# Down projection of a transformer block in seven products over halves, its summed activations made while gate and up are computed

## The chip, the cores and the metric

One core of one Trainium2 chip runs the whole block. The metric is the device time of one execution in microseconds (us), the median of several runs. The engines are TensorE (PE, with its weight loads as PEld), VectorE (DVE), ScalarE (ACT), GpSimd (POOL) and SyncE (SP), whose queue issues the DMAs of this kernel.

## The reference, cut to what matters

The block has a Hyena branch, a differential attention branch, an output projection and, last, a SwiGLU feed-forward. The change lies in the feed-forward alone:

```
hf = modulate(rmsnorm(x, g_ffn_pre), sh2, sc2)                      # 1024 positions x 1024
f  = (silu(hf @ w_gate) * (hf @ w_up)) @ w_down                     # 1024 x 2816, then 2816 x 1024
x  = x + g2 * rmsnorm(f, g_ffn_post)
```

All of it is in float32. Each product of two float32 matrices is computed as three matmuls on rounded halves: with a = a_hi + a_lo (a_hi rounded to TensorE's fp32r form, a_lo the rest), the kernel takes hi x hi, lo x hi and hi x lo. Making a hi takes one ScalarE copy, making a lo one VectorE subtraction.

## The kernel before

The kernel is written in a tile framework: code states tiles, rings of buffers (a tag with `bufs` slots) and operations. When the kernel is built, a list scheduler gives each engine its order by a model of the times, with the program's order as priority; on the chip each engine and the SP queue then run in that fixed order, each instruction waiting for what it needs. Loads are often issued far ahead of the place where the code states them, as far as a free slot of their ring allows.

The feed-forward has three stages around the change.

**Gate and up** (lines 1271 to 1370). The hidden size 2816 is NF = 22 tiles of 128. The result is computed transposed, hidden units on partitions, positions along the free axis in halves of 512. Tiles i and i + 11 (NH2 = 11) of gate (even j) and up (odd j) are taken together, and the 2 x 2 block product over halves of hidden units and of positions is made in seven products instead of eight, with sums of the weights made on VectorE (`prep`) and sums of the activations made once (`combos`). `product` runs 12 matmuls for each: 4 contraction tiles x 3 terms. `order` is (1, 5, 6, 3, 7, 2, 4); for the first NHS = 12 j's products 1 and 2 were made in an earlier head part that runs while the second half of the positions is still being prepared, so `order1` is (5, 6, 3, 7, 4). Several products accumulate on the same PSUM bank after its earlier content was copied out (b1, b5). `out_block(j, q, ...)` ends a block q (0, 1: first hidden half, 2, 3: second; even and odd: first and second half of positions): for gate it applies Silu, for up it calls `hidden`, which multiplies the two (VectorE), rounds the product to hi (ScalarE, line 1208), subtracts (VectorE) and stores both halves to DRAM (`ad[0]`, `ad[1]`). The weights come in as `wraw` tiles from a ring of 2 and are split into `whi` and `wlo` one product ahead (LA = 1).

**Down** (lines 1425 to 1459). For each half n of the positions and each half z of the outputs, 11 pieces q of two hidden tiles each are multiplied into four PSUM banks, one for each block b of 128 positions. A piece is `rows`: 4 blocks x 2 tiles x 3 terms = 24 matmuls with 512 output columns; a position block of the activations is the stationary operand, the weights move. `Pieces` loads w_down (512-byte runs, line 1032), splits 1024 columns at a time (line 126, line 127) and runs one piece ahead. The activations come back from DRAM already split (`down_load`), once for each n, into free slots of the rings xc, hfb, hfa and hfc. In all that is 2 x 2 x 11 x 24 = 1056 matmuls.

**End** (lines 1384 to 1467). `end_block` takes a finished bank: ScalarE sums the squares, VectorE multiplies by the gain (`om`). With both z done, `rows_rstd` makes the reciprocal root (12 small VectorE operations) and `turn` transposes back into feature-major form by small matmuls, adds x and stores. For n = 0 this (`final0`) runs between the pieces of n = 1. For n = 1 the last NLAST = 5 pieces of z = 1 are run block by block, so that the end of one block stands beside the matmuls of the next.

Of the kernel before, what the change touches and what calls it, by code (L numbers as in the profile page):

```python
# [17 lines left out]
P = 128  # L18
# [45 lines left out]
def block_kernel(tc, xT, ctxT, cvec, cT, wada1, wada, vecs, lamv, dbias, zT, fw1, fw2, fv, fw3, decay, mfs, mis, rope,  # L64
# [953 lines left out]
    ad = [[dp.tile([P, L], F32R, name=f"ad{j}{m}") for m in range(NF)] for j in range(2)]  # L1018
# [167 lines left out]


    KS2 = []
    for i in range(0, NH2 - 1, 2):
        KS2 += [(i, i + 1), (i + NH2, i + NH2 + 1)]  # L1190
    KS2.append((NH2 - 1, NF - 1))
    A_of = [{}, {}]

    def down_load(n, i):

        if n == 0:
            ring = (rt, "xc", 16) if i < 8 else (gp, "hfb", 16) if i < 16 else (rt, "hfa", 16)
        else:
            ring = (rt, "hfa", 16) if i < 2 else (fc, "hfc", 24) if i < 14 else (rt, "xc", 16)
        A_of[n][i] = split_tile(*ring)  # L1200
        for j in range(2):
            rawdma(A_of[n][i][j], ad[j][KS2[i // 2][i % 2]][:, n * 512:(n + 1) * 512])
# [22 lines left out]
    def out_block(j, q, t, hi=None):  # L1225


        i, mat = j // 2, j % 2
        if mat == 0:
            blk[i, q] = t if hi is None else hi  # L1230
            act(blk[i, q], t, AF.Silu)
        else:
            hidden(blk.pop((i, q)), t, t if hi is None else hi, i + NH2 * (q // 2), slice(q % 2 * 512, q % 2 * 512 + 512))
# [66 lines left out]
    pieces = [(n, z, q) for n in range(2) for z in range(2) for q in range(NH2)]  # L1300
    wd = Pieces(wdown, [(z, KS2[q]) for n, z, q in pieces])

# [5 lines left out]
    for g, (j, p) in enumerate(flat):  # L1308
# [21 lines left out]
        if j == NF - 1 and p in (7, 2):  # L1330
            wd.load()
            if p == 2:
                wd.split()
        product(b, wset.pop(g), XT[p], p in (1, 5) or (p == 2 and not head) or (p == 6 and j < NHS))
        ring = (lambda: xc("kp")) if j < NHS else p1_tile
# [3 lines left out]
        elif p == 2 and head:  # L1339
            out_block(j, 0, b, c11_tile())  # L1340
# [10 lines left out]
        elif p == 6:  # L1351
            keep[6] = evict(ring, b, "e")
        elif p == 3:
            tt(keep[6], keep[6], b, ALU.add)
            out_block(j, 1, keep[6])
        elif p == 7:
            if j < NHS:
                f7 = ring()
                tt(f7, p1[j], b, ALU.add)
            else:  # L1360
                f7 = evict(ring, b, "f")
            tt(keep[5], keep[5], f7, ALU.add)
            out_block(j, 3, keep[5])
        elif j < NHS:
            tt(p1[j], p1[j], b, ALU.add)
            out_block(j, 2, p1.pop(j))
        else:
            out_block(j, 2, b, ring())
        if 14 <= j < 18 and p in (5, 2):
            down_load(0, 2 * (j - 14) + (p == 2))  # L1370
# [32 lines left out]
    def final0():  # L1403
        scale_rows(0, rows_rstd(ssq[:, 2], D))
        yield
        for b in range(4):
            turn(0, b, bank2)
# [11 lines left out]
    def end_block(n, b, z, src):  # L1419
        sq = gp.tile([P, 512], F32, tag="c11", bufs=NC11, name="sq")  # L1420
        act(sq, src, AF.Square, accum_out=ssq[:, 2 + n, b, z:z + 1])
        om[n, b, z] = gp.tile([P, 512], F32, tag="p1", bufs=NHS, name="om")
        tt(om[n, b, z], src, gbc[z], ALU.mult)

    NLAST = 5
    kept = []
    for n, z, q in pieces:
        if (n, z) == (1, 1) and q >= NH2 - NLAST:
            kept.append(wd.next(len(kept) < 1) if len(kept) < 2 else
                        wd.keep(lambda: rt.tile([P, 512], F32R, tag="hfa", bufs=16, name="wkeep")))  # L1430
            continue
        if q == 0:
            acc = [bank() for b in range(4)]
        rows(acc, wd.next(), [A_of[n][2 * q + kk] for kk in range(2)], q == 0, q == NH2 - 1)
        if n == 0 and z == 0:
            if q < 4:
                for i in range(8 + 4 * q, min(12 + 4 * q, NF)):
                    down_load(0, i)
            else:
                for i in range(2):  # L1440
                    down_load(1, 2 * (q - 4) + i)
            if q == 3:
                down_gain()
        if n == 0 and z == 1 and 5 <= q < 9:
            for i in range(2):
                down_load(1, 14 + 2 * (q - 5) + i)
        if n == 1 and z == 0:
            if q == 0:
                load_x2(0)
                next(done)  # L1450
            elif q in (3, 4, 5, 6):
                next(done)
            elif q == 8:
                load_x2(1)
        if q == NH2 - 1:
            for b in range(4):
                end_block(n, b, z, acc[b])
            if z == 1:
                done = final0()

    for b in range(4):
        for i, w in enumerate(kept):
            q = NH2 - NLAST + i
            rows(acc, w, [A_of[1][2 * q + kk] for kk in range(2)], False, i == NLAST - 1, (b,))
        end_block(1, b, 1, acc[b])
        r = rows_rstd(ssq[:, 3, b:b + 1], D)
        turn(1, b, bank2, r)
# [103 lines left out]
```

## Time and profile before

| | |
|---|---|
| median of 3 runs | 1845.4 us (1843.83 to 1846.57) |
| profiled execution, its own time | 1844.04 us |
| its span from first to last instruction | 1842.3 us (1.7 us lie around it) |
| mean granted TensorE clock | 0.981 |
| TensorE busy, matmuls | 1750.0 us (95%), 8122 matmuls |
| VectorE busy | 1242.9 us (67%) |
| ScalarE busy | 752.6 us (41%) |

A matmul's busy time is longer than the distance to the next one, since matmuls overlap; how many end in a stretch says how fast TensorE runs. An idle time of an engine is put down to whatever released it last. The clock column tells which share of full speed TensorE was granted; 1.00 is 2.4 GHz, and the lower of its two levels is 1.2 GHz.

### The profile page before, as it was taken

How to read it: one execution, taken by the hardware profiler on the slowest of the kernel's cores; microseconds unless marked ns; L12 is line 12 of the kernel's file. 1: busy time of each engine (PE TensorE's matmuls, PEld its weight loads, DVE VectorE, ACT ScalarE, POOL GpSimd, SP SyncE). 2: the span in 40 equal slices, each digit the busy share in tenths (PEclk: the TensorE clock that was granted, in tenths of full speed). 3: DMA queues.
4: the chain of work that ended last, by engine and by line, in shares of the span. 5: the costliest groups of instructions: out<-in, count | busy, mean ns of one | idle time of the engine just before them, and what ended most of it. 6: DMA issues, size and time to landing. Idle time of an engine off the chain costs nothing.

```text
span 1842.3 us, 22476 instructions
## 1 busy us (share of the span) xinstructions
PE 1750.0 (95%) x8122; PEld 1404.0 (76%) x8122; DVE 1242.9 (67%) x2213; ACT 752.6 (41%) x1177; POOL 58.2 (3%) x63
## 2 busy tenths in 40 slices
PE   7899999999996999999998899989999999999997
PEld 3488777787875888887876687767778888788886
DVE  4887786777768589898858647876776565323334
ACT  3512323222232376667756357633334444222221
POOL 0000000000000211120100000000000000000000
PEclk9999999999997999999999899999999999999999
DMA  9244533324267733436438753433435324987432
GB/s 330 95 168 168 194 120 124 111 98 154 81 218 235 235 114 124 132 109 216 135 133 298 233 166 116 137 119 120 138 122 199 113 92 149 322 255 210 138 91 69
DMA packets 190111, 293.92 MB, mean 160 GB/s; under 512 B 15235, under 2 KB 110223, under 8 KB 188720
## 3 DMA queue, kind: packets, MB, share of 16 engines
q1 hardware_dynamic: 183776, 284.82, 47.0%
q10 hardware_dynamic: 6224, 7.66, 1.4%
q8 instruction: 64, 1.05, 0.3%
q14 instruction: 47, 0.39, 0.1%
HBM read 213.78 MB, written 78.64 MB: 159 GB/s over the span
## 4 chain that ended last, share of the span: by engine, by line
PE 70%; DVE 17%; DMA 7%; ACT 3%; issue 2%; SPq 0%; ACTq 0%; DVEq 0%
PE pj L1181 19%; PE ps L134 16%; PE ps L1043 15%; DVE pair L77 4%; PE S L804 4%; DVE quad L77 3%; PE pt L826 2%; PE psf L392 2%; PE psf L393 2%; DVE wlo L77 1%; PE psf L537 1%; PE pv L835 1%; PE psf L576 1%; PE psf L378 1%; DMA wraw<-wupf 1%
## 5 line engine op out<-in xcount | busy, mean ns | idle before, releaser
L77 DVE TENSOR_TENSOR wlo<-wraw,whi 128x1024 fp32r<-128x1024 f32 (+1 forms) x192 | 180.7, 949 | 286.8 <-ACT whi L126 130.9
L126 ACT CAST whi<-wraw 128x1024 fp32r<-128x1024 f32 (+1 forms) x119 | 118.1, 993 | 200.4 <-PE ps L1043 164.0
L134 PE MATMUL ps<-h_hi,wlo 128*128 128x512 f32 x640 | 173.6, 401 | 0.7 <-DVE wlo L77 0.7
L134 PE MATMUL ps<-h_hi,whi 128*128 128x512 f32 x640 | 173.9, 402 | 0.4 <-ACT h_hi L438 0.2
L134 PE MATMUL ps<-h_lo,whi 128*128 128x512 f32 x640 | 166.9, 393 | 0.0
L134 PEld LDWEIGHTS ps<-h_hi,wlo 128*128 128x128 f32 x640 | 119.4, 190 | 24.9 <-DVE wlo L77 1.1
L134 PEld LDWEIGHTS ps<-h_hi,whi 128*128 128x128 f32 x640 | 119.4, 191 | 24.1 <-ACT h_hi L438 1.2
L134 PEld LDWEIGHTS ps<-h_lo,whi 128*128 128x128 f32 x640 | 119.0, 188 | 24.1
L1181 PE MATMUL pj<-hfc,whi 128*128 128x512 f32 x528 | 131.7, 391 | 0.2 <-ACT p L1216 0.2
L1181 PEld LDWEIGHTS pj<-hfc,whi 128*128 128x128 f32 x528 | 98.9, 188 | 22.8 <-ACT p L1216 0.7
L804 PE MATMUL S<-KS,Q 128*128 128x512 f32 (+1 forms) x384 | 108.1, 377 | 2.9 <-DVE pr L808 2.7
L486 ACT COPY gt<-ps 128x512 f32<-128x512 f32 x56 | 32.9, 588 | 186.5 <-PE ps L134 149.2
L1181 PE MATMUL pj<-hfb,whi 128*128 128x512 f32 x352 | 93.4, 403 | 9.2 <-ACT whi L1173 9.2
L1181 PE MATMUL pj<-hfa,whi 128*128 128x512 f32 x352 | 90.1, 395 | 0.2 <-ACT whi L1173 0.2
L1181 PEld LDWEIGHTS pj<-hfb,whi 128*128 128x128 f32 x352 | 66.6, 191 | 27.5 <-ACT whi L1173 12.3
L804 PEld LDWEIGHTS S<-KS,Q 128*128 128x128 f32 x384 | 65.4, 191 | 16.8 <-DVE pr L808 9.0
L1181 PEld LDWEIGHTS pj<-hfa,whi 128*128 128x128 f32 x352 | 65.5, 188 | 15.5 <-ACT whi L1173 1.2
L1173 ACT CAST whi<-s 128x512 fp32r<-128x512 f32 x66 | 40.5, 621 | 77.0 <-DVE s L77 56.9
L1173 ACT CAST whi<-wraw 128x512 fp32r<-128x512 f32 x88 | 52.8, 618 | 44.7 <-PE pj L1181 34.0
L1181 PE MATMUL pj<-hfc,wlo 128*128 128x512 f32 x264 | 70.6, 389 | 0.0
L77 DVE TENSOR_TENSOR quad<-psf,xb 128x512 f32<-128x512 f32 x64 | 41.0, 682 | 35.9 <-ACT xb L250 35.9
L77 DVE TENSOR_TENSOR al<-pt,ah 128x512 fp32r<-128x512 f32 x80 | 52.2, 684 | 11.0 <-ACT ah L830 10.2
(492 smaller groups left out, 3566.4 us busy)
## 6 DMA issues: line engine op xcount, KB each, us to landing
wraw<-win SPq DMA_DIRECT2D x46, 512.0 KB, 4.1
wraw<-wdown SPq DMA_DIRECT2D x88, 256.0 KB, 3.4
wada_t<-wada SPq DMA_DIRECT2D x32, 512.0 KB, 8.0
wraw<-wgate SPq DMA_DIRECT2D x28, 512.0 KB, 3.3
wraw<-wupf SPq DMA_DIRECT2D x28, 512.0 KB, 3.9
ad<-p SPq DMA_DIRECT2D x52, 256.0 KB, 2.3
w_ada<-wada SPq DMA_DIRECT2D x16, 512.0 KB, 7.2
kspec<-quad SPq DMA_DIRECT2D x8, 1024.0 KB, 3.9
```

Of the source, the lines that this page charges most:

```text
L77: (eng or V).tensor_tensor(out=out, in0=a, in1=b, op=op)
L126: A.copy(out=hi, in_=raw)
L134: T.matmul(out=ps, lhsT=w[:, k * P:(k + 1) * P], rhs=xs[k][j], start=start and i == 0, stop=stop and i == len(seq) - 1)
L378: T.matmul(out=ps, lhsT=a[:, cs], rhs=b, start=i == 0, stop=i == 2)
L392: T.matmul(out=out, lhsT=mfm(part, r), rhs=gen[r][:, 0:256], start=True, stop=False)
L393: T.matmul(out=out, lhsT=mfm(pb, rb), rhs=gen[rb][:, 256:512], start=False, stop=True)
L486: A.copy(out=gt, in_=ps)
L804: T.matmul(out=S[:, :cn], lhsT=Q[j][:, i, qt * P:(qt + 1) * P], rhs=KS[i][:, c0:c0 + cn], start=j == 0, stop=j == 1)
L826: T.transpose(out=pt[:, b * 256 + qt * P:b * 256 + (qt + 1) * P], in_=av[qt][:, kt * P:(kt + 1) * P], identity=ident)
L1043: T.matmul(out=acc[b].rearrange("p (m c) -> p m c", m=4), lhsT=xs[kk][i == 1][:, b * P:(b + 1) * P], rhs=w[i == 2][kk], start=first and (k ...
L1173: A.copy(out=hi, in_=src)
L1181: T.matmul(out=ps, lhsT=w[a][:, k * P:(k + 1) * P], rhs=xs[k][b], start=start and i == 0, stop=stop and i == 11, skip_group_check=True)
```

## The change

The down product is treated as the gate and up products are: positions (n), hidden units (h: tiles i and i + 11) and outputs (z) are each cut into halves, and the 2 x 2 block product is made in seven products of 11 tiles each, in the order PR = (5, 1, 6, 7, 4, 3, 2). Each is 11 tiles x 4 blocks x 3 terms = 132 matmuls. Four of them use a sum of weight blocks (5, 6, 7, 4), made on VectorE from raw loads (`tk` is kept over 5, 6 and 4), and 5 and 7 load a second raw block for it. Products 1, 6, 7, 4 accumulate one behind the other on the same four PSUM banks; what they hold after 1 and after 6 is copied out on the way (m1, m6), and m5, m6 and m1 are added to later results. The order inside an item of two tiles is block by block.

`hidden` no longer rounds and splits. It stores the unsplit activations (xd[1], xd[4], xd[2]) and makes the four summed operands on VectorE (xd[5], xd[3], xd[6], xd[7]). For i < 6, whose block q = 0 was made in the head part, that block (a11) is read back from DRAM first. The seven operands are read back from DRAM unsplit, one product at a time (`x_load`, 8 tiles ahead), and split then (`x_prep`, 4 tiles ahead: a ScalarE copy and a VectorE subtraction for each 512 columns). Weights are loaded two items ahead (`w_load`) and prepared one ahead (`w_prep`). The last product runs its tiles 2 to 10 block by block; the half that ends last is now n = 0 (`final1` handles n = 1 during product 3).

```
-    ad = [[dp.tile([P, L], F32R, name=f"ad{j}{m}") for m in range(NF)] for j in range(2)]
+    xd = {p: [dp.tile([P, 512], F32, name=f"xd{p}{i}") for i in range(NF // 2)] for p in range(1, 8)}
...
-    def hidden(g, t, hi, k, sl):
+    hid = {}
+
+    def hidden(i, q, g, t, spare):
         tt(g, g, t, ALU.mult)
-        hi = hi.bitcast(F32R)
-        A.copy(out=hi, in_=g)
-        lo = g.bitcast(F32R)
-        tt(lo, g, f(hi), ALU.subtract)
-        rawdma(ad[0][k][:, sl], hi)
-        rawdma(ad[1][k][:, sl], lo)
+        put = lambda p, v: nc.sync.dma_start(out=xd[p][i], in_=v)
+        hid[i, q] = g, spare
+        if q == 0:
+            put(1, g)
+        elif q == 3:
+            put(4, g)
+            tt(spare, hid[i, 1][0], g, ALU.add)
+            put(5, spare)
+        elif q == 2:
+            put(2, g)
+            tt(spare, g, hid[i, 1][1], ALU.subtract)
+            put(3, spare)
+        if q == 3 and i < NHS // 2:
+            a11 = xc("a11")
+            nc.sync.dma_start(out=a11, in_=xd[1][i])
+            hid[i, 0] = a11, None
+        if (q == 3 or q == 0) and (i, 3) in hid and (i, 0) in hid:
+            (g1, s1), a11, sm = hid[i, 1], hid[i, 0][0], hid[i, 3][1]
+            tt(s1, sm, a11, ALU.subtract)
+            put(6, s1)
+            tt(g1, a11, g1, ALU.subtract)
+            put(7, g1)
...
+    PR = (5, 1, 6, 7, 4, 3, 2)
+    items = [(p, c) for p in PR for c in range((NH2 + 1) // 2)]
+    xseq = [(p, i) for p in PR for i in range(NH2)]
...
+    def w_load(t):
...
+        p, c = items[t]
+        h, z = {5: (0, 0), 1: (0, 0), 6: (1, 1), 7: (1, 1), 4: (1, 0), 3: (1, 1), 2: (1, 0)}[p]
+        raw = wp.tile([P, 1024], F32, tag="wraw", bufs=2, name="wraw")
...
+        for kk, i in enumerate(range(2 * c, min(2 * c + 2, NH2))):
+            get(raw[:, kk * 512:(kk + 1) * 512], h, z, i)
+            if p in (5, 7):
+                second.append(gp.tile([P, 512], F32, tag="hfb", bufs=16, name="wraw2"))
+                get(second[-1], 0, 1, i)
...
+    def w_prep(t):
...
+            if p == 5:
+                tk[i] = xc("tk")
+                tt(tk[i], second[kk], v, ALU.subtract)
+                v = tk[i]
+            elif p == 6:
+                tt(tk[i], v, tk[i], ALU.subtract)
+                v = tk[i]
+            elif p == 7:
+                tt(v, v, second[kk], ALU.subtract)
+            elif p == 4:
+                tt(v, v, tk[i], ALU.subtract)
...
+    def x_load(v):
+        if v < len(xseq):
+            p, i = xseq[v]
+            X[p, i] = [fc.tile([P, 512], d, tag="hfc", bufs=24, name="xw") for d in (F32R, F32)]
+            nc.sync.dma_start(out=X[p, i][1], in_=xd[p][i])
+
+    def x_prep(v):
...
+            A.copy(out=hi, in_=x)
+            tt(lo, x, f(hi), ALU.subtract)
...
+    for p in PR:
+        tail = p == PR[-1]
+        if p in (5, 1, 3, 2):
             acc = [bank() for b in range(4)]
...
+        cuts = [(0,), (1, 2, 3, 4, 5)] if tail else [(0,), (1,), (2,), (3,), (4, 5)]
+        for g, cs_ in enumerate(cuts):
+            for c in cs_:
+                w_load(it + 2)
+                w_prep(it + 1)
+                it += 1
+            tiles = [i for c in cs_ for i in range(2 * c, min(2 * c + 2, NH2))]
+            for i in tiles:
+                if not tail or g == 0:
+                    x_load(gx + 8)
+                    x_prep(gx + 4)
+                gx += 1
...
+            for b in range(4):
+                for q, i in enumerate(tiles):
+                    for u, (xj, wj) in enumerate(((0, 0), (1, 0), (0, 1))):
+                        T.matmul(out=acc[b], lhsT=X[p, i][xj][:, b * P:(b + 1) * P], rhs=W[p, i][wj],
...
+                if p == 5:
+                    m5[b] = evict(p1_tile, acc[b], "m5")
+                elif p == 1:
+                    m1[b] = evict(p1_tile, acc[b], "m1")
+                elif p == 6:
+                    m6[b] = evict(p1_tile, acc[b], "m6")
+                    tt(m6[b], m6[b], m5[b], ALU.add)
+                elif p == 7:
+                    tt(m5[b], m5[b], acc[b], ALU.add)
+                    end_block(1, b, 1, m5[b], m5[b])
+                elif p == 4:
+                    end_block(1, b, 0, acc[b], xc("om"))
+                elif p == 3:
+                    tt(m6[b], m6[b], acc[b], ALU.add)
+                    end_block(0, b, 1, m6[b], m6[b])
+                else:
+                    tt(m1[b], m1[b], acc[b], ALU.add)
+                    end_block(0, b, 0, m1[b], m1[b])
+                    turn(0, b, bank2, rows_rstd(ssq[:, 2, b:b + 1], D))
```

## Rows read from the trace of the kernel before

**Rows 1.** The page: span, and part 1, busy time by engine.
```profile
span 1842.3 us, 22476 instructions
PE 1750.0 (95%) x8122; PEld 1404.0 (76%) x8122; DVE 1242.9 (67%) x2213; ACT 752.6 (41%) x1177; POOL 58.2 (3%) x63
```

**Rows 2.** Busy time by window: head, gate and up (two parts), down with end.
```profile
core 0: us, PE busy (x) PEld busy (x) DVE busy (x) ACT busy (x) POOL busy (x), PEclk, DMA share, GB/s
1115.00:1207.00 92.00, 84.17 (x378) 66.52 (x376) 75.99 (x143) 67.47 (x122) 0.00 (x0) 0.98 0.39 132
1207.00:1378.00 171.00, 166.41 (x708) 133.58 (x709) 123.30 (x198) 62.94 (x108) 0.00 (x0) 0.99 0.36 122
1378.00:1574.00 196.00, 195.75 (x854) 159.65 (x853) 115.55 (x186) 86.80 (x151) 0.00 (x0) 1.00 0.42 145
1574.00:1842.30 268.30, 256.60 (x1158) 210.05 (x1156) 88.93 (x157) 63.73 (x91) 0.00 (x0) 0.99 0.60 178
```

**Rows 3.** Busy time by window inside the down stage, same columns.
```profile
1600.00:1650.00 50.00, 50.00 (x220) 40.89 (x219) 13.71 (x13) 12.71 (x18) 0.00 (x0) 1.00 0.85 269
1700.00:1750.00 50.00, 50.00 (x238) 41.74 (x237) 17.05 (x30) 14.40 (x17) 0.00 (x0) 1.00 0.48 137
```

**Rows 4.** Instruction groups of the gate and up stage, 1207 to 1574 us.
```profile
L77 DVE TENSOR_TENSOR p<-p,p 128x512 f32<-128x512 f32 x30 | 20.6, 686 | 6.9 <-ACT p L1216 6.7
L77 DVE TENSOR_TENSOR p<-p,p 128x512 fp32r<-128x512 f32 x23 | 15.4, 684 | 3.4 <-ACT p L1208 3.4
L77 DVE TENSOR_TENSOR s<-wraw 128x512 f32<-128x512 f32 x21 | 14.5, 690 | 24.1 <-DMA wraw<-wupf 13.1 <-DMA wraw<-wgate 11.0
L1208 ACT CAST p<-p 128x512 fp32r<-128x512 f32 x24 | 14.8, 622 | 29.1 <-DVE p L77 28.8
L1216 ACT COPY p<-pj 128x512 f32<-128x512 f32 x40 | 23.3, 584 | 29.5 <-PE pj L1181 29.4
```

**Rows 5.** What PE waited for, 1221 to 1574 us: total, times, longest.
```profile
PE pj L1181 <- ACT whi L1173: 4.2, 6, 1.4
PE pj L1181 <- ACT p L1216: 0.2, 1, 0.2
```

**Rows 6.** DMA issues, 1207 to 1378 us: count, KB each, median us to landing.
```profile
wraw<-wgate SPq DMA_DIRECT2D x12, 512.0 KB, 3.3
```

**Rows 7.** Timeline at the entry of the down stage: start, duration.
```profile
1563.66 2.04 SPq L1032 DMA_DIRECT2D wraw<-wdown  x4
1572.11 0.93 SPq L1032 DMA_DIRECT2D wraw<-wdown  x2
1574.21 3.79 PE L1043 MATMUL ps<-whi,xc 128*128 128x512 f32 x16
```

**Rows 8.** Instruction groups of the down stage, 1574 us to the end.
```profile
L77 DVE TENSOR_TENSOR wlo<-wraw,whi 128x1024 fp32r<-128x1024 f32 x40 | 49.0, 1225 | 142.5 <-PE ps L1043 78.0 <-ACT whi L126 42.6 <-DMA x<-x2d 13.1
L77 DVE TENSOR_TENSOR om<-ps,gbc 128x512 f32<-128x512 f32 x16 | 11.0, 690 | 15.4 <-ACT sq L86 15.4
L126 ACT CAST whi<-wraw 128x1024 fp32r<-128x1024 f32 x40 | 42.1, 1053 | 148.1 <-PE ps L1043 139.8 <-DMA wraw<-wdown 8.4
```

**Rows 9.** Timeline, three VectorE splits in a row in gate and up.
```profile
1308.59 1.89 DVE L77 TENSOR_TENSOR wlo<-s,whi 128x512 fp32r<-128x512 f32 x3
```

**Rows 10.** DMA traffic and issues, 1574 to 1690 us.
```profile
DMA packets 40022, 32.55 MB, mean 281 GB/s; under 512 B 1984, under 2 KB 31567, under 8 KB 40015
q1 hardware_dynamic: 40015, 32.46, 92.3%
wraw<-wdown SPq DMA_DIRECT2D x42, 256.0 KB, 4.2
hfc<-ad SPq DMA_DIRECT2D x24, 256.0 KB, 5.8
```

**Rows 11.** Timeline of the last block: its squares, gain and transposes.
```profile
1830.67 0.60 ACT L86 ACTIVATE sq<-ps 128x512 f32<-128x512 f32 x1 [8.68 <-PE ps L1043]
1834.92 3.21 PE L1397 MATMUL pt<-dg,om 128*128 128x128 f32 x16 [4.35 <-DVE dg L83]
```

More of the change, by code (lines that the diff above doesn't have):

```diff
@@ new lines, in w_prep @@
+    def w_prep(t):
+        if t >= len(items):
+            return
+        p, c = items[t]
+        raw, second = wraws.pop(t)
+        tiles = range(2 * c, min(2 * c + 2, NH2))
+        srcs = []
+        for kk, i in enumerate(tiles):
+            v = raw[:, kk * 512:(kk + 1) * 512]
+            if p == 5:
[9 more added lines that the diff above has]
+                tt(v, v, tk[i], ALU.subtract)
+            srcs.append(v)
+        if len(tiles) == 2 and not (p == PR[-1] and c >= 3):
+            hi, lo = [wp.tile([P, 1024], F32R, tag=u, bufs=2, name=u) for u in ("whi", "wlo")]
+            if p in (5, 6):
+                for kk in range(2):
+                    sl = slice(kk * 512, (kk + 1) * 512)
+                    split_to((hi[:, sl], lo[:, sl]), srcs[kk], V)
+            else:
+                split_to((hi, lo), raw, V)
+            for kk, i in enumerate(tiles):
+                W[p, i] = [v[:, kk * 512:(kk + 1) * 512] for v in (hi, lo)]
+        else:
+            for kk, i in enumerate(tiles):
+                W[p, i] = split_tile(rt, "hfa", 16)
+                split_to(W[p, i], srcs[kk], V)
@@ L1367, in block_kernel @@
         else:
-            out_block(j, 2, b, ring())
-        if 14 <= j < 18 and p in (5, 2):
-            down_load(0, 2 * (j - 14) + (p == 2))
+            out_block(j, 2, b, ring)
+        if j == NF - 1 and p in (2, 4):
+            for v in range(4):
+                x_load(4 * (p == 4) + v)
+            if p == 2:
+                for v in range(4):
+                    x_prep(v)
     om.clear()
@@ L1401, in turn, with final1 @@
                               in_=x2.rearrange("p (k c) -> p k c", k=4))
[L1403 to L1404 removed]
+    def final1():
+        scale_rows(1, rows_rstd(ssq[:, 3], D))
         yield
         for b in range(4):
[L1407 removed]
+            turn(1, b, bank2)
             yield
@@ L1417, in load_x2, with end_block @@
                                   in_=x2d[:, 4 * z:4 * z + 4, n * 512 + b * P:n * 512 + (b + 1) * P])
-    def end_block(n, b, z, src):
+    def end_block(n, b, z, src, dst):
         sq = gp.tile([P, 512], F32, tag="c11", bufs=NC11, name="sq")
         act(sq, src, AF.Square, accum_out=ssq[:, 2 + n, b, z:z + 1])
[L1422 to L1432, printed above, removed]
-            acc = [bank() for b in range(4)]
[L1434 to L1442, printed above, removed]
-                down_gain()
[L1444 to L1449, printed above, removed]
-                next(done)
[L1451 to L1459, printed above, removed]
```

69 lines of the change are left out of this document (41 added, 28 removed).

## The prediction, made before the change was run

> **What bounds the kernel now.** First the page: of 1842.3 us TensorE's matmuls are busy 95% and VectorE 67% [rows 1]. That is a mean over stages, so next comes busy time by stage [rows 2]. The change touches the last three: the head of gate and up, where VectorE is busy 76 of 92 us and TensorE 84; the rest of gate and up, where TensorE loses 4.6 of 171 us and then 0.3 of 196; and the down stage with its end, 268.3 us, where VectorE is busy only 89 and ScalarE 64. In the middle of the down stage TensorE never rests: 220 matmuls end in 50 us at a granted clock of 1.00, the upper level, 2.4 GHz [rows 3]. So it is bound by the number of its matmuls, at 50 / 220 = 0.2273 us each. Its 1056 matmuls are 240.0 us of the 268.3; the rest is the 96 small matmuls of the transposes and the chain after the last block. DMA is the other thing that is full there: from 1574 to 1690 us the queue's packets fill 92.3% of the engines at 281 GB/s [rows 10], and TensorE still does not wait.
>
> **Matmuls removed.** Seven products of 132 are 924 matmuls for 1056. 132 x 0.2273 = 30.0 us less, all of it in a stage where TensorE sets the time. The new matmuls have the same size and as many weight loads each, so I take the same pace. This is the whole gain; everything below says how much of it is given back.
>
> **Hidden in gate and up.** Each of 44 blocks loses a ScalarE cast of 0.622 us and a VectorE subtraction of 0.684 us and keeps the multiplication [rows 4]. The seven summed operands cost four VectorE operations for each of 11 pairs, again 44, at the 0.686 us of the multiplication. So VectorE's work is equal in sum but moves: the head loses 6 subtractions (4.1 us), the pairs i < 6 gain one each. ScalarE's 27 us lie beside matmuls and are worth nothing. Stores fall from 88 to 77. New is a read of a11 for i < 6: the load is queued on SP behind the store of X5, and two VectorE subtractions wait for it. A load of twice its size lands after 3.3 us [rows 6]. Behind these subtractions on VectorE stand the splits for the next product, and TensorE waits for those. The nearest row is VectorE's wait for weight loads in this stage, 24.1 us over 21 operations [rows 4], for which TensorE lost 4.2 us in 6 waits on the casts that follow [rows 5]: 0.2 us lost for 1.1 us waited. Six a11 waits run from 0 (the list scheduler puts other work ahead of them) to some 4 us each, 24 in all; with up to 4 us of gain from the head as the bound on the other side. I take +1.5, near the row.
>
> **Entry of the down stage.** Before, its first matmul follows the last of gate and up directly, since activations came split and early; the first weights were loaded from 1563.66 us, the second from 1572.11, when the `wraw` slots came free [rows 7]. The first item now is four loads of 256 KB and four VectorE operations (two sums, two subtractions, 2.7 us) beside two casts, and four activation tiles must be read and split. The slots of the activations (XT[3], XT[6]) come free over 10 us ahead, so these are hidden; the second item, 1 MB issued at about 1572, takes 3.7 us at 281 GB/s plus the 2.7 us and is wanted 24 matmuls (5.5 us) after 1574.2. That is 0 to 8 us late counting the queue in front of it; I take +2.5.
>
> **VectorE and ScalarE in the products.** Prices: 0.69 us for 512 columns and 1.225 for a split of 1024 [rows 8], 0.63 for 512 when they follow each other [rows 9]. Each product splits 11 activation tiles. Adding the weight splits, the sums and the operations on finished banks, product 5 has 33 operations of 512 (22.8 us); product 1 has 12 and 5 wide ones (14.4); product 6 has 37 (25.5); 7 has 31 and 5 wide (27.5); 4 has 27 and 5 (24.8); 3 has 28 and 5 (25.4); 2 has 32 and 3 (25.8) beside its small ones. TensorE needs 30.0 us for each, so all of this lies beside matmuls, but product 7 fills 92% of its time (84% at the shorter spacing). ScalarE stays near half (22 casts of about 0.62 us, copies of 0.584 [rows 4]). The nearest row for a stage with VectorE this full is the head: VectorE 83%, TensorE 91% [rows 2]. If TensorE lost 9% in products 6, 7 and 4 that would be 8 us; with nothing lost, 0. The head also waits on statistics and transposes, which these products do not, so I take +2.
>
> **DMA.** The stage moves 77 activation tiles, 99 weight blocks and 32 blocks of x and output, 208 x 262 KB = 54.5 MB; before it was 88, 88 and 32, the same amount. At the 281 GB/s of [rows 10] that is 194 us against 210 us of matmuls. By product: 5 and 7 need 33 blocks, 30.8 us against 30.0; product 4 with the load of x for the second half 28.0; product 3 with x and output 35.5; the others 20.5. The parts above 30 are borrowed from the prefetch of eight activation tiles and two weight items. Loads take 4.2 to 5.8 us to land there [rows 10], against two items, 10.9 us, from a slot's reload to its next use. The 512-byte pieces move at no better than 137 / 0.48 = 285 GB/s [rows 3]. Bounds 0 and 10 us; I take +1.
>
> **The chained banks.** After products 1 and 6 a copy out (0.584 us, ScalarE), after 7 a VectorE addition (0.69) must be through before the next product writes that bank. The last three tiles run block by block, so block 0 is finished 27 x 0.2273 = 6.1 us before the product ends, and block 3 is written again 18 matmuls, 4.1 us, into the next. The gate and up stage chains products on a bank too, and TensorE waited 0.2 us in all for the copies out [rows 5]. I take +0.5, bounds 0 and 7.
>
> The Trainium skill speaks against this edit: "Perfetto Trace Analysis", section Optimizing Tensor Performance (Matmuls), wants independent matmul groups to rotate through PSUM banks so that the evacuation of one overlaps the next group's matmuls. The row just named does not show that loss in chained products; by the rule the three seams would cost what the rival below works out, by the row nothing.
>
> **The end.** The last block's chain gains one VectorE addition in front of its squares (0.69 us); from 1830.67 on the rest is as before, with its 4.35 us wait of TensorE [rows 11]. Per block 27 matmuls (6.1 us) instead of 30 now cover a chain longer by that addition. I take +1.0, bounds 0.7 and 4.
>
> **Sum.** -30.0 + 1.5 + 2.5 + 2 + 1 + 0.5 + 1.0 = -21.5 us. Against the profiled execution's own time of 1844.0 us (span 1842.3) that is 1822.5. The median shown, 1845.4, is 1.4 above it, so the forecast is 1824.
>
> **The rivals.** First, the weight slots hold the sum products: with `wraw` at two slots, an item of product 7 keeps its slot through four loads (1 MB, 3.7 us, landing after 5.8), two subtractions and a wide split on ScalarE and VectorE (1.4 + 1.05 + 1.23), 9.5 us and whatever it waits in VectorE's queue, against 10.9. Two us over in each of the 18 items or so of 5, 7 and 4 would be up to 16 us: 1832 to 1840. For it: VectorE is then nearly full and SP's queue is in order; against it, TensorE did not wait at 281 GB/s.
>
> Second, each chained seam is exposed: four evictions one behind the other (4 x 0.6 us) at three seams, 7 us in place of 0.5: 1830. The rule cited above would have it so; the chained products of [rows 5] speak against it.
>
> Third, the a11 reads stall VectorE in front of the splits, 4 us in each of six pairs, with the other costs at twice what I took: -30 + 24 + 14 = +8 at worst, no change (1842 to 1849) near its middle. Against it, the slack of VectorE there, 48 of 171 us [rows 2].
>
> Fourth, slower: VectorE runs in step with ScalarE. If every subtraction waits for its own cast, a 512-column split costs 0.62 + 0.69 = 1.31 us and a wide one 2.28. Products 5, 6, 7 and 4 then take 36, 39, 40 and 37 us instead of 30, 33 us more; with the other terms +3, 1848. It decides against the change once those four lose over 21 us beyond what I took. For it: VectorE's waits on the cast `whi` are 42.6 us in the old stage [rows 8], though it had nothing else to do then; against it, three splits in a row at 0.63 us each [rows 9], with the casts ahead.
>
> **How the numbers follow.** The forecast as summed, between 1814 (all costs near their lower bounds) and 1831: 0.62. Weight slots, 1831 to 1840: 0.16. Seams, 1830: 0.06. No change by a11: 0.06. Slower, VectorE in step: 0.10. Faster is the first three, 0.84; about 0.2% (3.7 us) is what a measurement can tell from no change. The range that leaves out no more than 2 in 10 reaches over the forecast, the seams and most of the slots' case: 1813 to 1838.
>
> **What would show it right or wrong.** Right: 924 matmuls of 512 columns in the down stage at 0.227 us, stage and end together some 245 us, VectorE near 170 us busy in it, waits at the entry of a few us, none at the seams after 1, 6 and 7. The slots' rival shows as TensorE waiting for `whi` or `wlo`, and ScalarE for `wraw`, inside products 5 and 7; the seams as TensorE waiting on the copies out m1 and m6; the a11 rival as VectorE waiting on `a11` and a gate and up stage above 367 us; the last as VectorE waiting on casts while TensorE waits for it. The forecast is wrong if these waits together pass 20 us, or if the pace of the new matmuls, with activation tiles and weights fresh from VectorE, is not 0.227 us.

## The result, and the profile after

The changed kernel takes 1822.2 us (median of 4 runs, 1817.09 to 1825.07) where the one before took 1845.2 beside it (4 runs, 1843.83 to 1846.57): a ratio of 0.9871, interval [0.9854, 0.9889], 23 us faster. The profiled execution took 1822.15 us, 21.9 less than that of before. The page of the changed kernel, span and busy time by engine, answers to [rows 1]:

```profile
span 1820.3 us, 22426 instructions
PE 1725.2 (95%) x7990; PEld 1380.8 (76%) x7990; DVE 1319.6 (72%) x2357; ACT 769.9 (42%) x1229; POOL 58.2 (3%) x63
```

TensorE has 132 matmuls less, 7990 for 8122, and VectorE 77 us more. Busy time by stage answers to [rows 2], with the same columns and cuts:

```profile
1115.00:1207.00 92.00, 86.06 (x385) 69.56 (x383) 73.35 (x137) 64.37 (x117) 0.00 (x0) 0.98 0.34 115
1207.00:1378.00 171.00, 165.92 (x703) 132.40 (x704) 125.69 (x202) 54.08 (x92) 0.00 (x0) 0.99 0.37 129
1378.00:1574.00 196.00, 196.00 (x855) 160.14 (x854) 117.34 (x191) 77.52 (x134) 0.00 (x0) 1.00 0.34 115
1574.00:1820.30 246.30, 230.75 (x1029) 184.98 (x1027) 165.51 (x298) 102.20 (x179) 0.00 (x0) 0.98 0.72 213
```

The down stage begins within a microsecond of where it did; the whole gain is in the last row, 246.3 for 268.3 us. VectorE's work there went from 89 to 165.5 us. The entry, in the timeline (start, duration), answers to [rows 7]: the last matmul of gate and up, then the first of the down stage with no wait between.

```profile
1573.85 1.07 PE L1181 MATMUL pj<-hfc,wlo 128*128 128x512 f32 x4
1574.76 0.61 PE L1534 MATMUL ps<-whi,xw 128*128 128x512 f32 x2
```

Next the same view cut at the first matmul of each product, in the order 5, 1, 6, 7, 4, 3 and, to the last big matmul, 2:

```profile
1574.76:1607.30 32.54, 32.54 (x138) 25.32 (x137) 27.22 (x46) 16.72 (x30) 0.00 (x0) 1.00 1.04 312
1607.30:1637.20 29.90, 29.90 (x134) 24.75 (x133) 15.40 (x21) 13.13 (x22) 0.00 (x0) 1.00 1.08 306
1637.20:1668.80 31.60, 30.57 (x134) 24.53 (x133) 24.71 (x40) 15.17 (x27) 0.00 (x0) 1.00 0.89 263
1668.79:1700.99 32.20, 30.37 (x133) 24.54 (x132) 19.88 (x29) 11.48 (x19) 0.00 (x0) 1.00 0.70 217
1700.99:1732.60 31.61, 30.95 (x132) 24.55 (x133) 23.05 (x34) 16.42 (x33) 0.00 (x0) 1.00 0.62 185
1732.60:1767.48 34.88, 34.02 (x165) 27.96 (x164) 23.25 (x44) 18.45 (x32) 0.00 (x0) 1.00 0.78 225
1767.48:1807.50 40.02, 37.89 (x183) 29.24 (x181) 26.27 (x72) 10.11 (x21) 0.00 (x0) 1.00 0.28 78
```

A count takes in matmuls that only reach into a window, so it can stand one or two above 132. Product 1 runs at full pace: 29.92 us from its first matmul to the next product's, 0.2267 for each of its 132, while DMA moves 306 GB/s. Products 6, 7 and 4 take 1.7, 2.3 and 1.7 us more than that; products 5, 3 and 2 have small matmuls of broadcasts and transposes among theirs. What TensorE waited for in the stage (total, times, longest):

```profile
PE pt L1477 <- DVE dg L83: 6.0, 4, 5.1
PE ps L1534 <- DVE wlo L77: 2.5, 3, 1.0
PE ps L1534 <- ACT hfa L1023: 1.0, 1, 1.0
PE ps L1534 <- DVE p L77: 0.9, 1, 0.9
PE ps L1534 <- ACT whi L1023: 0.8, 1, 0.8
```

The first is the chain after a block of the last product; the others are weights not split in time, and one seam, where a product's first matmul waits for a bank that the product before has left. What VectorE waited for in the same stage says why:

```profile
DVE wraw L77 <- DMA wraw<-wdown: 20.4, 11, 4.2
DVE tk L77 <- DMA wraw<-wdown: 9.7, 6, 5.3
```

The 4.2 us wait, in the timeline at the end of product 7:

```profile
1683.56 1.22 DVE L77 TENSOR_TENSOR wlo<-wraw,whi 128x1024 fp32r<-128x1024 f32 x1
1684.80 0.37 SPq L1319 DMA_DIRECT2D wraw<-wdown  x1
1685.15 1.04 ACT L1023 CAST whi<-wraw 128x1024 fp32r<-128x1024 f32 x1
1689.61 0.69 DVE L77 TENSOR_TENSOR wraw<-wraw,wraw 128x512 f32<-128x512 f32 x1 [4.23 <-DMA wraw<-wdown]
1690.82 1.22 DVE L77 TENSOR_TENSOR wlo<-wraw,whi 128x1024 fp32r<-128x1024 f32 x1
1692.10 0.50 PE L1534 MATMUL ps<-wlo,xw 128*128 128x512 f32 x1 [0.93 <-DVE wlo L77]
```

Read it as a loop. The split of 1683.56 frees a weight slot; the load of the item after next goes out at once (1684.80) and lands 4.7 us later. VectorE's next operation in its fixed order is the sum on that load, so VectorE stands idle until 1689.61, though the split that TensorE needs first (1690.82) has had its cast since 1686.2. TensorE waits 0.93 us for it, and 0.90 more at the seam behind product 7 (1700.99), together most of the 2.3 that this product loses. The wait for `wlo` in product 6 (1.00 us, at 1650.01) and that in product 4 (0.53, at 1724.76) have the same shape: a sum on the eleventh tile's weights that waits for its load (1.22 us at 1648.05) stands ahead of a split that TensorE wants. In product 4, where that split had had its cast since 1719.2:

```profile
1722.27 0.69 DVE L77 TENSOR_TENSOR wraw<-wraw,tk 128x512 f32<-128x512 f32 x1 [3.20 <-DMA wraw<-wdown]
1723.48 1.22 DVE L77 TENSOR_TENSOR wlo<-wraw,whi 128x1024 fp32r<-128x1024 f32 x1
```

### The profile page after: what moved, and what is told of

It is laid out like the page before. It is cut to its first block, busy times and chain, and to the rows that moved or that the text cites. A ratio compares the mean times of both kernels' runs of the same rounds, so it can differ in the third digit from the quotient of the medians.

```text
span 1820.3 us, 22426 instructions
## 1 busy us (share of the span) xinstructions
PE 1725.2 (95%) x7990; PEld 1380.8 (76%) x7990; DVE 1319.6 (72%) x2357; ACT 769.9 (42%) x1229; POOL 58.2 (3%) x63
## 4 chain that ended last, share of the span: by engine, by line
PE 68%; DVE 19%; DMA 8%; ACT 3%; issue 2%; SPq 0%; ACTq 0%; DVEq 0%
PE pj L1181 19%; PE ps L134 17%; PE ps L1534 8%; DVE pair L77 4%; PE ps L1043 4%; PE S L804 4%; DVE quad L77 3%; PE pt L826 2%; DVE wlo L77 2%; PE psf L392 2%; DMA wraw<-wdown 2%; PE psf L393 2%; PE psf L537 1%; PE pv L835 1%; PE psf L576 1%
## 5 line engine op out<-in xcount | busy, mean ns | idle before, releaser
L77 DVE TENSOR_TENSOR wlo<-wraw,whi 128x512 fp32r<-128x512 f32 (+1 forms) x174 | 158.2, 920 | 161.6 <-ACT whi L126 88.0
L1534 PE MATMUL ps<-whi,xw 128*128 128x512 f32 x528 | 164.1, 392 | 1.8 <-DVE p L77 0.9
L1534 PEld LDWEIGHTS ps<-whi,xw 128*128 128x128 f32 x528 | 98.5, 188 | 24.7 <-ACT whi L1023 1.8
L1534 PE MATMUL ps<-wlo,xw 128*128 128x512 f32 x264 | 103.5, 393 | 2.7 <-DVE wlo L77 2.5
L126 ACT CAST whi<-wraw 128x1024 fp32r<-128x1024 f32 (+1 forms) x78 | 74.9, 962 | 51.8 <-PE ps L1043 25.4
```

The lines of the kernel that those rows point to most:

```text
L77: (eng or V).tensor_tensor(out=out, in0=a, in1=b, op=op)
L126: A.copy(out=hi, in_=raw)
L1534: T.matmul(out=acc[b], lhsT=X[p, i][xj][:, b * P:(b + 1) * P], rhs=W[p, i][wj], start=p in (5, 1, 3, 2) and (g, q, u) == (0, 0, 0), stop=l ...
```

## The experiments

Totals of single executions mix in stages far ahead of the change: the down stage began between 1565 and 1575 us in the profiled executions of these kernels, those with no edit ahead of it included. So beside each time stands **the stage**, from the first matmul of the down products to the end of the span: 268.1 us before (1574.21 to 1842.3), 245.5 after. From a repeat (245.8) and from a kernel with no edit in that stage (247.2) differences under about 1.7 us are not told apart.

The theory: the matmuls fell as forecast, and what is given back in the stage is lost where VectorE's order puts a sum that waits for a weight load ahead of a split that TensorE needs. The rivals: the activations' path, the chained banks, the read-back of a11, or a pace below 0.227 us.

**The changed kernel again.**

> The changed kernel once more, to pair with the two behind it. Both theories: 1817 to 1825 us, about 1.3% below the kernel before; TensorE again waits some us inside products 6, 7 and 4. If the spread of its four earlier times (8 us) comes from how weight loads land, the runs spread over 4 us or more again; if it was chance, they lie within 2 us.

Measured: 1819.0 us, ratio 0.9859 [0.9833, 0.9886]; stage 245.8 us; the same waits. The four times spread over 10.7 us, but so do the kernel before's twelve (9.9 us), so the spread says nothing about the weight loads.

**The sums on GpSimd.** In `w_prep`, all four sums:

```
-                tt(v, v, second[kk], ALU.subtract)
+                tt(v, v, second[kk], ALU.subtract, G)
```

> The 44 sums of weight blocks are made on GpSimd, which is idle here and takes about 1.34 us for such an operation (an estimate from its 16 subtractions of that size earlier in the kernel); VectorE loses 30 us of work and all waits for the weight loads of products 5, 6, 7 and 4. Theory (the wait in front of the splits costs): TensorE's waits in 6, 7 and 4 fall to under 2 us, time 3 to 6 us lower. Rival (VectorE full): the same sign, time 3 to 6 us lower too, but with VectorE's busy time per product the thing that changed; told apart by the third slot, which leaves VectorE as full. Third possibility: GpSimd is late itself, and TensorE waits for it, time 5 us or more longer.

Measured: 1834.2 us, 0.9947 [0.9927, 0.9966]; stage 260.7 us, 15 more than after: the third of the possibilities came true. The groups of this stage show two reasons, GpSimd's time and what became of VectorE's:

```profile
L77 POOL TENSOR_TENSOR tk<-wraw,tk 128x512 f32<-128x512 f32 x11 | 17.2, 1597 | 36.3 <-DMA wraw<-wdown 35.7 <-DVE xw L77 0.6
L77 DVE TENSOR_TENSOR xw<-xw 128x512 fp32r<-128x512 f32 x74 | 63.1, 875 | 20.6 <-ACT xw L1375 20.6
L77 DVE TENSOR_TENSOR wlo<-tk,whi 128x512 fp32r<-128x512 f32 x20 | 21.7, 1109 | 14.8 <-ACT whi L1023 14.8
```

The waits for loads did leave VectorE, but a sum takes 1.6 us for 0.69, and VectorE's own splits slowed from 0.686 and 0.688 us. So the run doesn't tell the theory from its rivals; it only shows that this way out is closed.

**The kernel before, 132 matmuls fewer.** `rows` leaves out two of the six (tile, term) steps of a piece until 33 are gone:

```
+            steps = [u for u in steps if u not in ((0, 1), (1, 1))[:drop]]
...
+        cut = 0 if q in (0, NH2 - 1) or left == 0 else min(2, left)
```

> The kernel before, with 132 of the 1056 matmuls of the down projection left out (the lo-activation terms of 16 pieces and half of one more), all loads and splits kept: the first term of the sum by itself. Theory: 132 x 0.2273 = 30.0 us less, 1815 us. Rival (matmuls hide other work already, so that leaving them out uncovers DMA or splits): 20 to 27 us less, with new waits in the first half of the stage, where DMA is full.

Measured: 1817.6 against 1842.8 us, 0.9864 [0.9842, 0.9886]: 25.2 us less (21 to 29), not 30, as the rival had it. The window from 1574 to 1690 us:

```profile
1574.00:1690.00 116.00, 111.30 (x477) 88.64 (x476) 41.51 (x54) 38.17 (x53) 0.00 (x0) 1.00 0.96 285
```

TensorE's waits for the pieces' weights in this window:

```profile
PE ps L1045 <- ACT whi L126: 4.0, 5, 1.3
```

At 285 GB/s the pieces that were made shorter caught up with their weights: 4.0 us of waits that [rows 3, 10] didn't have. The cover that hid the loads was worth some of the 30 us. The pace itself is settled by the run without the weights' path, below.

**A third weight slot.** A third slot of 1024 columns doesn't fit in memory (its pool would take 58 kB per partition, 55 are left), so every third item is loaded into two free tiles of the ring `hfa`:

```
+        if t % 3 == 2:
+            raw = [rt.tile([P, 512], F32, tag="hfa", bufs=16, name="wraw3") for _ in range(2)]
+        else:
```

> Every third weight item of the down stage is loaded into two free 512-column tiles, so that a load can be issued one item earlier. Theory (VectorE stands waiting for a weight load with a split or addition behind it that TensorE needs): VectorE's waits on weight loads, 29 us in the changed kernel's down stage, fall to under 12, TensorE's listed waits on splits and additions there from 5.2 us to under 2, and the time is 3 to 5 us below the changed kernel, 26 to 29 below the kernel before. Rival (VectorE is full): its work grows by some 3 us, waits stay, time as the changed kernel or 1 to 2 us longer.

Measured: 1812.6 against 1846.1 us, 0.9824 [0.9798, 0.9849]; stage 241.5 us, 4.0 less. TensorE's waits for `wlo` are gone, and products 6 and 4 take 29.9 us each, the full pace; VectorE's waits for loads fell only from 30.1 to 25.8 us (under 12 expected), but the longest from 5.3 to 3.1 us. Product 7 takes 35.4 us: one new wait stands at the seam after product 6. ScalarE's order around it in the timeline:

```profile
1662.78 1.55 ACT L1218 COPY p<-ps 128x512 f32<-128x512 f32 x3
1668.66 0.62 ACT L1023 CAST hfa<-wraw 128x512 fp32r<-128x512 f32 x1 [4.33 <-DMA wraw<-wdown]
1670.65 0.57 ACT L1218 COPY p<-ps 128x512 f32<-128x512 f32 x1
1671.28 0.72 PE L1538 MATMUL ps<-whi,xw 128*128 128x512 f32 x2 [3.48 <-ACT p L1218]
```

The busy times of this kernel during and after that wait, columns as above:

```profile
1667.50:1671.30 3.80, 0.32 (x3) 0.02 (x1) 3.40 (x6) 2.64 (x5) 0.00 (x0) 1.00 0.65 183
1671.30:1675.00 3.70, 3.70 (x10) 2.96 (x11) 2.51 (x4) 3.25 (x6) 0.00 (x0) 0.60 1.06 328
1675.00:1679.00 4.00, 4.00 (x18) 3.21 (x17) 2.90 (x5) 0.00 (x0) 0.00 (x0) 0.94 1.10 316
```

It is the same fault on another engine: a cast that waits 4.33 us for a weight load stands in ScalarE's order ahead of the fourth block's copy out, and product 7 can't write that bank. The wait costs twice: behind it the granted clock reads 0.60, part of the stretch at the lower of the two levels, and 10 matmuls are counted where 16 fit.

**The loads of x later.** For n = 0 they go to a ring whose slots come free later:

```
+                x2t[n, b, z] = xc("x2") if n == 0 else gp.tile([P, 512], F32, tag="hfb", bufs=16, name="x2")
```

> The eight loads of x for the half that ends last take slots that come free only with product 4, so they leave the queue of products 6 and 7. Theory (weight loads land late because of what stands beside them in DMA and in SP's queue): VectorE's waits on weight loads fall by a third from 29 us, time 1 to 3 us below the changed kernel, 24 to 26 below the kernel before. Rival (a weight load's time is its own, 3.4 us or more from issue to landing, whatever is beside it): no difference of more than 1 us.

Measured: 1814.7 against 1846.1 us, 0.983 [0.9814, 0.9847]; stage 243.7 us, 1.8 less, hardly more than can be told. TensorE's waits for `wlo` are 3.2 us, VectorE's longest for `wraw` still 4.2, and its waits for loads 27.3 us where 30.1 were, not a third less. Product 7 now takes 29.9 us, but products 6 and 4 still 31.7 and 32.0. The loads of x in the queue are at most a part of what makes the weights late.

**Without the weights' path.** Loads, sums and splits of all items but the first are left out:

```
+        if t:
+            for i in range(2 * c, min(2 * c + 2, NH2)):
+                W[p, i] = W[5, i % 2]
+            return
```

> Left out: all weight loads, sums and splits of the down stage but those of the first item, whose two tiles serve for all; activations are read and split as in the changed kernel. Theory: the waits inside products 6, 7, 4 and 3 vanish and only the end's remain, 7 to 9 us below the changed kernel, 30 to 32 below the kernel before. Rival (the activations' reads and splits fill VectorE and ScalarE): at most 3 us below the changed kernel.

Measured: 1807.5 us, 0.9796 [0.9779, 0.9812]; stage 235.1 us, 10.4 less than after (7 to 9 expected). TensorE's only wait in it is the last chain:

```profile
PE pt L1483 <- DVE dg L83: 6.2, 4, 5.1
```

This is the floor of the seven products: 924 x 0.2273 = 210.0, some 10.5 for the 80 transposes ahead of the last block's, 2 for broadcasts and 12.9 from the last big matmul to the end make 235.4. Products 1, 6, 7 and 4 take 29.92 us each, and in the kernel before an undisturbed piece of 24 matmuls takes 5.44 us: 0.2267 a matmul in both, so the pace is that of before. The changed kernel loses 10.4 us above it. Where, matmuls counted in 12.5 us show. First a window of the changed kernel, inside product 2:

```profile
1774.76:1787.26 12.50, 11.32 (x45) 7.57 (x44) 6.65 (x15) 3.82 (x7) 0.00 (x0) 1.00 0.31 89
```

And one of the kernel without the weights' path:

```profile
1608.19:1620.69 12.50, 12.50 (x57) 10.36 (x56) 3.99 (x6) 3.01 (x5) 0.00 (x0) 1.00 0.40 119
```

The busy column hides most of it: 11.32 of 12.50 us, but 45 matmuls for 57, 2.7 us lost. The Trainium skill, "Perfetto Trace Analysis", section Identifying the Most-Contended Engine, says as much: TensorE is to be judged by the arithmetic it does and the busy share of its weight loads, not by the busy share of its matmuls; here that column falls from 10.36 to 7.57. The rows behind the loss, from the timeline of the changed kernel:

```profile
1781.87 0.62 ACT L1023 CAST hfa<-wraw 128x512 fp32r<-128x512 f32 x1 [1.76 <-DMA wraw<-wdown]
1782.54 1.23 PE L1534 MATMUL ps<-hfa,xw 128*128 128x512 f32 x3 [1.04 <-ACT hfa L1023]
```

The last product's second group, tiles 2 to 10, wants the weights of five items within its first block, 27 matmuls or 6.1 us, and loads of them land only then.

**Without the activations' path.** Loads and splits of all but the first four tiles are left out:

```
+            if v >= 4:
+                X[xseq[v]] = X[5, v % 4]
+                return
```

> Left out: all reads and splits of activations in the down stage but those of the first four tiles, which serve for all; weights as in the changed kernel. VectorE loses 50 us of work and DMA 19 MB. Theory (what costs is the wait for weight loads, two slots at a time): 0 to 3 us below the changed kernel, VectorE still waiting 15 us or more on weight loads. Rival (VectorE full, DMA full): 6 to 9 us below it.

Measured: 1812.9 us, 0.982 [0.9799, 0.984]; stage 238.5 us, 7.0 less than after. That is in the rival's range, and more than the theory allowed an innocent path. VectorE's waits for weight loads are as long as ever:

```profile
DVE wraw L77 <- DMA wraw<-wdown: 24.8, 10, 4.3
DVE tk L77 <- DMA wraw<-wdown: 6.2, 9, 2.3
```

Yet TensorE waits only 1.6 us beside the last product's chains, and products 6, 7 and 4 take 29.9 us each. The weight loads landed hardly sooner, 3.7 us after issue (median) instead of 3.9, though DMA moved 145 GB/s instead of 227. So the load waits alone harm nothing in these products; they harm when the 43 us of activation splits on VectorE, and the 38 us of casts ahead of them on ScalarE, fill what time is left. Which of these two counts more is not told apart. It takes both, waits and work, and the theory as first put was too narrow.

**Rotated banks.** Every product starts on fresh banks, and VectorE adds what the chain added:

```
-        if p in (5, 1, 3, 2):
+        if True:
...
+                    un[b] = xc("un")
+                    tt(un[b], m1[b], acc[b], ALU.add)
```

> The chains are undone: products 6, 7 and 4 start in fresh banks, and the running sums are kept in memory by VectorE (12 more additions of 0.69 us, 8 copies out by ScalarE fewer... four, after product 6). Judged by the length from the first matmul of the down stage to the end of the span, 245.5 and 245.8 us in two executions of the changed kernel. Theory (the chained banks cost next to nothing; what TensorE waits for at the seam after product 7 is VectorE standing behind a weight load): the same within 2 us, or up to 2 us longer for the added work. Rival (the seams are exposed, 7 us): 4 to 6 us shorter.

Measured: 1818.2 against 1842.9 us, 0.9863 [0.9843, 0.9884]; stage 246.7 us against 245.5 and 245.8. TensorE has no seam wait left, but waits 4.2 us for `wlo` in place of 2.5, behind 7.7 us more of VectorE's work:

```profile
PE ps L1534 <- DVE wlo L77: 4.2, 4, 2.0
```

The longest of these waits, 2.00 us, is followed by a granted clock of 0.65 over 4 us (1703 to 1707), with 10 matmuls counted where 17.6 fit. So this run shows that rotating doesn't pay here, but not what the chained banks cost by themselves. Two runs above show that: without the weights' path and without the activations' path the banks are chained as ever, and products 6, 7 and 4 run at 29.9 us. The chained banks cost nothing of their own. The rule of the Trainium skill that was weighed in the prediction ("Perfetto Trace Analysis", section Optimizing Tensor Performance, Matmuls) is put for independent groups, and rotating brings nothing in this stage; whether it would at the third slot's seam, where a copy out comes late, was not tried.

**No read-back of a11.** The pair takes a tile at hand instead:

```
-            nc.sync.dma_start(out=a11, in_=xd[1][i])
-            hid[i, 0] = a11, None
+            hid[i, 0] = g, None
```

> For the pairs i < 6, the block that the changed kernel reads back from DRAM (a11) is not read; another block that is still in memory stands in its place. All sums are made, with that block. Theory (the read-back costs nothing, the scheduler having put other work ahead of it): from the first matmul of product 5 on all contraction tiles at about 1207 us to the first of the down stage the same within 1 us (367.3 before, 367.3 after), time as the changed kernel within 2 us. Rival (my term of 1.5 us, up to 24): 1.5 us or more shorter there.

Measured: 1820.6 against 1842.9 us, 0.9876 [0.9858, 0.9894]. The gate and up stage from its products on is 367.6 us, against 367.3 after and 366.8 before. The read-back costs nothing that can be told. (The expectation's 367.3 for the kernel before is 366.8 when both ends are taken from its trace.)

**Third slot and later loads together.** Both edits, as shown above; nothing else changes.

> The third weight slot and the late loads of x together. Their stage lengths alone were 241.5 and 243.7 us against 245.5 and 245.8 of the changed kernel. Theory (both shorten the same wait, that of VectorE for weight loads): less than the sum of the two, 240 to 241.5. Rival (two costs of their own): 239.5 or less.

Measured: 1817.3 against 1842.9 us, 0.9861 [0.9844, 0.9877]; stage 243.1 us, not less than the third slot alone and outside what either side expected. The seam wait is there again (3.06 us), and behind it the clock at 0.86 over 12 us. The two don't add up.

**These two, and the last two items of a product in groups of their own.** To the edits above:

```
-        cuts = [(0,), (1, 2, 3, 4, 5)] if tail else [(0,), (1,), (2,), (3,), (4, 5)]
+        cuts = [(0,), (1, 2, 3, 4, 5)] if tail else [(0,), (1,), (2,), (3,), (4,), (5,)]
```

> As e11_slot_and_x_late, and only the eleventh tile of each product, not the last three, runs block by block. The last weight item is then wanted 24 matmuls (5.5 us) later, but a finished bank has 2.0 us instead of 6.1 us until it is written again. Theory (the waits left in products 6, 7 and 4 are for the last weight item): 1 to 3 us shorter than e11. Rival (the seams need the time): 1 to 4 us longer, with TensorE waiting on copies out and additions.

Measured: 1811.3 against 1842.9 us, 0.9827 [0.9812, 0.9842]; stage 238.3 us, 4.8 less than without the last edit (1 to 3 expected) and 3.2 above the floor. TensorE's waits before the last chain:

```profile
PE ps L1538 <- DVE p L77: 1.7, 1, 1.7
PE ps L1538 <- DVE xw L77: 0.6, 1, 0.6
```

**That last edit alone.** With items 4 and 5 in one group, block by block, TensorE wants the splits of both within its first block, 9 matmuls or 2.0 us; in groups of their own the second is wanted a whole group later.

> The changed kernel with one edit: only the eleventh tile of each product runs block by block, not the last three. Weight slots and loads of x as in the changed kernel. Theory (in the last group the last weight item is wanted 6 matmuls, 1.4 us, after its start instead of 24, and VectorE, behind its weight loads, is late for it; this is most of the 5 us of waits in products 6, 7 and 4): from the first matmul of the down stage to the end 241 to 243 us against 245.5 and 245.8. Rival (the shorter group helps only where the third slot lets loads come earlier): 245 us or more, with TensorE waiting on the splits as before, or at the seams.

Measured: 1811.9 us (5 runs, 1808.69 to 1813.28) against 1841.8, 0.9837 [0.9821, 0.9853]; stage 241.2 us, 4.3 less than after. TensorE's waits before the last chain:

```profile
PE ps L1534 <- ACT p L1218: 2.0, 1, 2.0
PE ps L1534 <- ACT hfa L1023: 0.8, 1, 0.8
PE ps L1534 <- DVE xw L77: 0.2, 1, 0.2
```

No wait for `wlo` is left, with two slots and the same sums: VectorE's wait for `wraw` falls from 20.4 to 15.3 us, its longest to 3.4. Products 6, 7 and 4 take 30.1, 29.9 and 30.3 us; the 2.0 us wait is a new seam behind product 1.

The stage came out as the theory had it, but not by the reason given. The waits that are gone were for splits of earlier tiles (4 and 5 in product 6, 8 and 9 in products 7 and 4), which TensorE wants at the start of a group in either grouping, and not for the eleventh tile's. At the end of products 7 and 4 VectorE still has the eleventh tile's sum ahead of the split of tiles 8 and 9. The sum now waits 2.73 and 3.16 us for its load instead of 4.23 and 3.20, and the split is through 1.7 and 1.1 us before TensorE wants it, where it came 1.0 and 0.6 us late. Why VectorE is that much earlier no run shows.

One line is worth what a slot is worth. This kernel and the one with all three edits beat both kernels of the case, the changed one by 0.2 to 0.4% of its time. The stage, 4.3 and 7.2 us shorter, says it more clearly than the totals, whose ratio intervals overlap with that of the changed kernel's repeat.

## Why the prediction was right

The forecast was 1824 us within 1813 to 1838; 1822.2 was measured. By its own steps:

| step | forecast, us | measured, us |
|---|---|---|
| 132 matmuls less | -30.0 | -30.0, at the pace of the run without the weights' path |
| a11, work moved in gate and up | +1.5 | +0.4, within what can be told; without the read-back 0.3 more, not less |
| entry | +2.5 | about 0.7: 105 matmuls in the first 25 us for 108 without the weights' path |
| VectorE in the products, DMA, seams | +3.5 | 5.7 in products 6, 7 and 4 |
| the end | +1.0 | 1.3 for the last chain, and 2.7 at the start of the last group |

The right column is counted above the floor of the new stage. Of its 10.4 us there the 1.3 that the table leaves out lie in product 3, which takes 34.9 us for the 33.5 without the weights' path. The old stage lost 4.0 above its own floor (268.1 less 240.0, 10.5, 2 and 11.6), which the new one no longer has: -30.0 + 0.4 + 0.7 + 5.7 + 1.3 + 2.7 + 1.3 - 4.0 = -21.9, as the profiled executions differ. So the forecast's -21.5 came out right with a gain left out (the old stage's own losses, 4.0) against costs put too low (8.5 for 12.1). That the two errors cancel to 0.4 us is luck; that 30 us come in and some 8 to 12 go back is not.

**Matmuls and bound.** Right: 7990 matmuls at the old pace, VectorE 165.5 us busy (forecast near 170), stage and end 245.5 us (some 245). DMA at 306 GB/s in product 1 cost TensorE nothing, as [rows 10] let expect, and the 281 and 285 GB/s of the DMA term were not the most it moves.

**The entry** was over-sized. No wait of TensorE is listed in product 5, and the first matmul followed the last of gate and up as in [rows 7].

**The products** were under-sized, and the row chosen for them, the head's full VectorE, was not the mechanism. Product 7, put at 27.5 us of VectorE's time and 92% full, has 19.9 of 32.2 us in its window and still loses 2.3. What the traced waits have in common is VectorE's order: an operation on a late load in front of one that is due. But order alone does not lose the time either: in the last experiment products 7 and 4 keep it and take 29.9 and 30.3 us. It does where the work leaves too little time to catch up, as the run without the activations' path shows. The first rival had named the slots and the queue; it came true in small, some 5 us instead of up to 16, and through VectorE rather than through slots alone, as the run with two slots and shorter groups shows. (Its price doesn't follow from its own figures: 2 us in each of 18 items are 36, not 16.)

**The end** had the term for the last chain nearly right, as the timeline of the last block shows beside [rows 11]:

```profile
1812.56 3.75 PE L1477 MATMUL pt<-dg,p 128*128 128x128 f32 x16 [5.11 <-DVE dg L83]
```

The wait is 5.11 us for 4.35. But the step left out that a group of nine tiles run block by block wants all their weights within its first block. The timeline shows that wait; no run takes it away alone.

**The other rivals.** The seams cost 0.9 us, a11 nothing. VectorE in step with ScalarE, the slower case, did not come: its waits for `whi` are 11.1 us where [rows 8] had 42.6, and for all casts of weights and activations 24.6. (That rival's +3 is -30 and 33 alone; with the other terms, as it says, it would be +9.5.)

Three things stay open: what VectorE's order is worth by itself, since no run changes it and nothing else; the 3.2 us between the best stage and the floor; and why the stage's start differs by up to 10 us between the profiled executions.

## What to carry to other kernels

Where matmuls set the time, their count times the pace of an unstalled window gives the gain; what is given back is found not in busy shares alone but in fixed orders, by asking of each operation that waits for a load what stands behind it on its engine. Running a group block by block means that the weights of the whole group are wanted within the first block, so keep groups as short as the prefetch. A third buffer and a shorter group bought the same 4 us; the second cost one line.

## What the runs showed of the hardware that was not expected

VectorE's operations on two operands in SBUF slow down while GpSimd works. The means above, 875 and 1109 ns, mix two cases. In the run with the sums on GpSimd, 93 such operations of 512 columns met no GpSimd operation and took 0.68 to 0.69 us; of 16 that lay wholly inside GpSimd's, 15 took 1.1 to 1.8 us. GpSimd's own took 1.3 us alone and about 1.7 beside them. Two additions with an operand in PSUM lay inside GpSimd operations and took 0.68 us. One of each kind:

```profile
1633.94 12.75 POOL L77 TENSOR_TENSOR tk<-wraw,tk 128x512 f32<-128x512 f32 x8 [35.48 <-DMA wraw<-wdown]
1638.67 1.78 DVE L77 TENSOR_TENSOR wlo<-tk,whi 128x512 fp32r<-128x512 f32 x1
1706.68 4.76 POOL L77 TENSOR_TENSOR wraw<-wraw,tk 128x512 f32<-128x512 f32 x3 [0.45 <-DMA wraw<-wdown]
1710.22 0.68 DVE L77 TENSOR_TENSOR p<-p,ps 128x512 f32<-128x512 f32 x1
```

The Trainium skill, "SBUF — State Buffer", section Who interferes with whom, has this: a VectorE instruction with two SBUF inputs contends with a GpSimd instruction that reads SBUF. The trace agrees, with 1.78 us against 0.68.

A wait of TensorE can cost more than its length: after 3.48 us with nothing to do the granted clock was 0.60 for 3.7 us and 0.94 for 4 more; after 3.06 us it was 0.86 over 12 us; after 2.00 us, with rotated banks, it was 0.65 over 4 us; after 2.03 us in the last experiment it stayed at 1.00. So in these runs the length of the wait does not settle whether the clock falls.
